# Staged norm and rotary chains for queries and keys, and Q/K projections scattered through the block of an eight-core hybrid layer

## The chip, the cores and the metric

The kernel runs on all 8 cores of one Trainium2 chip, each core on one of 8 batch entries, without traffic between cores. The metric is the time on the device of the slowest core. The profile lists the cores as two dies of four. In some executions, of nine of the fourteen kernels here, cores of one die (of both in the last run of the changed kernel) ran at a lower granted TensorE clock and the time was longer: in one run of the changed kernel four cores had 0.853 to 0.859 and took 2738.1 to 2774.8 us, the other four 0.972 to 0.976 and 2513.1 to 2524.3 us. Such runs are called slow, and only fast runs are compared. Names below: PE is TensorE, ACT is ScalarE, DVE is VectorE, POOL is GpSimd.

## The reference, cut to what matters

```python
h = _rmsnorm(x, g_mix)                                   # x: (8, 4096, 1024) float32
z = einsum(h, w_in)                                      # B_c | C_c | V_c | Q | K | V_a | gate_c | gate_a
y_c = (B_c * causal_dwconv3(C_c * V_c)) @ w_conv_out
q = _apply_rope(_rmsnorm(q, q_norm), cos, sin)           # per sub-head of 64; the same for k
o = (softmax(q1 k1) - lam * softmax(q2 k2)) @ v          # 4 heads, chunk-causal
y_a = (_rmsnorm(o, sub_norm) * (1 - lam_init)) @ w_attn_out
x = x + (sigmoid(gate_c) * y_c + sigmoid(gate_a) * y_a) @ w_o
x = x + SwiGLU(_rmsnorm(x, g_ffn))                       # 1024 -> 2816 -> 1024
```

## The kernel before

A core walks through 8 tiles of 512 tokens. For tile j it does conv and gates, w_o, the Q/K/V projection of tile j+2, FFN up and FFN down. The attention of tile j+1 is woven in as steps: two score matmuls, one exponential on ACT, eight P·V matmuls, spread evenly over the other matmuls. "Unit" means one PSUM bank's worth of projection (8 matmuls); there are 3 such banks (`psD`), used in rotation. Work that must wait for another engine is put off by `defer(n, f)`: f is put into the engines' instruction streams at the end of the n-th unit, counting the present one. In the trace what stands behind a wait in an engine's stream waits too: near 1402 us of the kernel before, ACT stands 2.81 us for a result of VectorE, and a ready activation and exponential behind it start only at 1404.3 and 1404.7 us. So the place in the stream is what this change is about.

The chain of one Q or K unit, and the order of the block:

```python
    act(lambda: A.activation(out=scr[:, s1, 0:512], in_=psD[bk][:], func=AF.Square), [("ps", bk)], [("scr", s1)])
    dve(lambda: V.tensor_tensor(
        out=s23, in0=ps3, in1=tabs[:, 2 * qk, t, :].unsqueeze(1).to_broadcast([128, 8, 64]), op=ALU.mult),
        [("ps", bk), ("tab", qk)], [("scr", s2)])
    dve(lambda: V.tensor_reduce(out=ss8, in_=s13, axis=AX.X, op=ALU.add), [("scr", s1)], [("ss8", pb)])
    dve(lambda: V.tensor_scalar(out=ss8, in0=ss8, scalar1=1.0 / 64, scalar2=EPS, op0=ALU.mult, op1=ALU.add),
        [("ss8", pb)], [("ss8", pb)])
    pool(lambda: G.tensor_tensor(out=rs8, in0=ss8, in1=mhalf[:], op=ALU.pow), [("ss8", pb), "mhalf"], [("rs8", pb)])
    sw = psD[bk][:].rearrange("p (g two d) -> p g two d", g=8, two=2)[:, :, ::-1, :]
    tb = tabs[:, 2 * qk + 1, t, :].rearrange("p (two d) -> p two d", two=2)
    dve(lambda: V.tensor_tensor(
        out=scr[:, s1, 0:512].rearrange("p (g two d) -> p g two d", g=8, two=2), in0=sw,
        in1=tb.unsqueeze(1).to_broadcast([128, 8, 2, 32]), op=ALU.mult),
        [("ps", bk), ("tab", qk)], [("scr", s1)])
    pool(lambda: G.tensor_tensor(out=scr[:, s2, 0:512], in0=scr[:, s2, 0:512], in1=scr[:, s1, 0:512], op=ALU.add),
         [("scr", s1), ("scr", s2)], [("scr", s2)])
# [cut: fin = final product yq = s2 * rs8 on VectorE; tr = 4 transposes of yq into a bank, copied to qT or kT]
    defer(1, fin)
    defer(3, tr)

def proj_qkv(j, free):
# [cut: rotary tables, ones column of V]
    for hbs, kind in ((HB_Q, 0), (HB_K, 1), (HB_V, 2)):
        for t in range(4):
            bk = tm_unit(hbs, t, j)
            if kind < 2:
                qk_chain(j, kind, t, bk)
# [cut: V copied out by ScalarE]
            unit_end()
```

The end of a head of attention (its epilogue), after the products with PSUM on VectorE:

```python
for q in range(4):
    act(lambda q=q: A.activation(out=yq[:, yi, q * 128:(q + 1) * 128], in_=wv[:, q, :], func=AF.Square,
                                 accum_out=ss[:, q:q + 1]), [("scr", w)], [("yq", yi), ("ess", e)])
dve(...)    # [cut] ss / 128 + eps
pool(...)   # [cut] rs = ss ** -0.5
# [cut: fin = wv * rs on VectorE, tr = 4 transposes and a copy]
defer(1, fin)
defer(3, tr)
```

Of the kernel before, what the change touches and what calls it, by code (L numbers as in the profile page):

```python
# [154 lines left out]
def build_program():  # L155
# [8 lines left out]
    with contextlib.ExitStack() as es:  # L164
# [6 lines left out]
        NDB = 3  # L171
        psD = [es.enter_context(nc.psum_tensor("psD%d" % i, [128, 512], F32)) for i in range(NDB)]
# [30 lines left out]
        st8 = sb("st8", [128, 2, 24], F32)  # L203
# [12 lines left out]
        def program(S_):  # L216
# [6 lines left out]

            def new_scr():
                return rot("scr", NSCR)

            def new_bank():
                return rot("bank", NDB)

# [42 lines left out]
            def defer(n, fn):  # L272
                later.append([n, fn])
# [8 lines left out]

            def flush_later():
                while later:
                    later.pop(0)[1]()
# [6 lines left out]
            SEQ_A = list(range(0, 6))  # L292
            SEQ_C1 = list(range(6, 28))
            SEQ_C2 = list(range(28, NHB))
            wseq = [(0, b) for b in SEQ_A]
            for j in range(NST):
                wseq += [(j, b) for b in SEQ_C1]
                if j + 2 < NST:
                    wseq += [(j + 1, b) for b in SEQ_A]
                wseq += [(j, b) for b in SEQ_C2]  # L300
            NW = len(wseq)
            ring = {"issued": 0, "cast": 0, "used": 0, "rel": [False] * NW, "cur": {}, "wb": []}
# [18 lines left out]
            def pump():  # L321
                while ring["issued"] < NW:
                    k = ring["issued"]
                    p, b = wseq[k]
                    if is_f32(k):
                        if k - NSTG >= ring["cast"]:
                            break
                        i = k % NSTG
                        S_.dma("sp", [lambda: nc.sync.dma_start(
                            out=stg_view(i), in_=wblk_d[b].rearrange("p (h c) -> p h c", h=4))],  # L330
                            [], stg_keys(i), ("stg", i))
                    else:
                        if k >= NSLOT and not ring["rel"][k - NSLOT]:
                            break
                        sl = k % NSLOT
                        n = hbw(b)
                        S_.dma("sp", [lambda: nc.sync.dma_start(out=wring[:, sl, 0:n], in_=wsc_d[b][:, 0:n])],
                               [("wsc", b)], [("w", sl)], ("wr", sl))
# [8 lines left out]
            def cast(k):  # L347
                assert k == ring["cast"] and (k < NSLOT or ring["rel"][k - NSLOT]), k
                p, b = wseq[k]
                i, sl = k % NSTG, k % NSLOT  # L350
                sv = stg_view(i)
                dst = wring[:, sl, :].rearrange("p (h c) -> p h c", h=4)
                if k % 2 == 0:
# [3 lines left out]
                ring["cast"] += 1  # L357
                ring["wb"].append((b, sl))

            def ready(k):  # L360

                while ring["cast"] <= k and ring["cast"] < NW and is_f32(ring["cast"]):
                    cast(ring["cast"])
                    pump()
                    do_wb(1)

            def ahead(k):
                if k < NW and is_f32(k) and (k < NSLOT or ring["rel"][k - NSLOT]):
                    ready(k)

            def wuse(b):

                if b in ring["cur"]:
                    return ring["cur"][b] % NSLOT
                k = ring["used"]
                assert wseq[k][1] == b, (wseq[k], b)
                if is_f32(k):
                    ready(k)
                    ahead(k + 1)
                else:  # L380
                    do_wb(0)
                    while ring["cast"] < NW and ring["cast"] <= k:
                        ring["cast"] += 1
                pump()
                assert ring["issued"] > k
                ring["used"] += 1
                ring["cur"][b] = k
                return k % NSLOT

            def wfree(b):  # L390
                k = ring["cur"].pop(b)
                if any(w[0] == b for w in ring["wb"]):
                    do_wb(0)
                ring["rel"][k] = True
# [12 lines left out]
            def norm_pre(t):  # L407
# [5 lines left out]
                dve(lambda: V.tensor_scalar(out=ss, in0=ss, scalar1=1.0 / D, scalar2=EPS, op0=ALU.mult, op1=ALU.add),  # L413
                    [("ss", t)], [("ss", t)])
                pool(lambda: G.tensor_tensor(out=rs, in0=ss, in1=mhalf[:, 0:1], op=ALU.pow),  # L415
                     [("ss", t), "mhalf"], [("rs", t)])
                dve(lambda: V.tensor_scalar(out=xn[:, t, :], in0=src, scalar1=rs, scalar2=None, op0=ALU.mult),
                    [("xt", t), ("rs", t)], [("xn", t)])

            def norm_T(t, gcol0, dst, dkey):  # L420
                bk = new_bank()
                bv = bankbf(bk).rearrange("p (c k) -> p c k", c=8)
                for kc in range(8):
# [5 lines left out]
                    [("ps", bk), "cst"], [(dkey, t)])  # L429

# [89 lines left out]
            def qk_chain(j, qk, t, bk):  # L520
                s1, s2 = new_scr(), new_scr()
                pb = rot("st8", 2)
                yi = rot("yq", NYQ)
                ps3 = psD[bk][:].rearrange("p (g d) -> p g d", g=8)
                s13 = scr[:, s1, 0:512].rearrange("p (g d) -> p g d", g=8)
                s23 = scr[:, s2, 0:512].rearrange("p (g d) -> p g d", g=8)
                ss8, rs8 = st8[:, pb, 0:8], st8[:, pb, 8:16]
                act(lambda: A.activation(out=scr[:, s1, 0:512], in_=psD[bk][:], func=AF.Square), [("ps", bk)], [("scr", s1)])
# [3 lines left out]
                dve(lambda: V.tensor_reduce(out=ss8, in_=s13, axis=AX.X, op=ALU.add), [("scr", s1)], [("ss8", pb)])  # L532
                dve(lambda: V.tensor_scalar(out=ss8, in0=ss8, scalar1=1.0 / 64, scalar2=EPS, op0=ALU.mult, op1=ALU.add),  # L533
                    [("ss8", pb)], [("ss8", pb)])
                pool(lambda: G.tensor_tensor(out=rs8, in0=ss8, in1=mhalf[:], op=ALU.pow), [("ss8", pb), "mhalf"], [("rs8", pb)])  # L535
                sw = psD[bk][:].rearrange("p (g two d) -> p g two d", g=8, two=2)[:, :, ::-1, :]
                tb = tabs[:, 2 * qk + 1, t, :].rearrange("p (two d) -> p two d", two=2)
# [6 lines left out]

                def fin():
                    dve(lambda: V.tensor_tensor(
                        out=yq[:, yi, :].rearrange("p (g d) -> p g d", g=8), in0=s23,
                        in1=rs8.unsqueeze(2).to_broadcast([128, 8, 64]), op=ALU.mult),
                        [("scr", s2), ("rs8", pb)], [("yq", yi)])

                def tr():
                    b2 = new_bank()
# [6 lines left out]
                    else:  # L559
                        c0 = j * T + t * 128  # L560
                        act(lambda: A.copy(out=kT[:, :, c0:c0 + 128], in_=bv), [("ps", b2)], [("kT", j * 4 + t)])

                defer(1, fin)
                defer(3, tr)

            def proj_qkv(j, free):
                make_tabs(j)
                pool(lambda: G.memset(Vs[:, j * 4:j * 4 + 4, :].rearrange("p k (h d) -> p k h d", d=VW)[:, :, :, 128:129], 1.0),
                     [], [("V", j * 4 + t) for t in range(4)])
                for hbs, kind in ((HB_Q, 0), (HB_K, 1), (HB_V, 2)):  # L570
                    for t in range(4):
                        bk = tm_unit(hbs, t, j)
                        if kind < 2:
                            qk_chain(j, kind, t, bk)
                        else:
                            act(lambda t=t, bk=bk: A.copy(
                                out=Vs[:, j * 4 + t, :].rearrange("p (h d) -> p h d", d=VW)[:, :, 0:128],
                                in_=psD[bk][:].rearrange("p (h d) -> p h d", h=NH)), [("ps", bk)], [("V", j * 4 + t)])
                        unit_end()
                    if free:  # L580
                        wfree(hbs[0])
                        wfree(hbs[1])
# [7 lines left out]
            def attention_steps(j):  # L590
# [31 lines left out]
                def epilogue(h):  # L622
# [25 lines left out]
                    yi = rot("yq", NYQ)  # L648
                    for q in range(4):
                        act(lambda q=q: A.activation(out=yq[:, yi, q * 128:(q + 1) * 128], in_=wv[:, q, :], func=AF.Square,  # L650
                                                     accum_out=ss[:, q:q + 1]), [("scr", w)], [("yq", yi), ("ess", e)])
                    dve(lambda: V.tensor_scalar(out=ss, in0=ss, scalar1=1.0 / 128, scalar2=EPS, op0=ALU.mult, op1=ALU.add),  # L652
                        [("ess", e)], [("ess", e)])
                    pool(lambda: G.tensor_tensor(out=rs, in0=ss, in1=mhalf[:, 0:4], op=ALU.pow), [("ess", e), "mhalf"], [("ers", e)])  # L654

                    def fin():
# [3 lines left out]
                            [("scr", w), ("ers", e)], [("yq", yi)])  # L660

                    def tr():
                        b2 = new_bank()
                        bv = bankbf(b2)[:, 0:512]
                        for q in range(4):
# [4 lines left out]
                            [("ps", b2), "sn08"], [("onT", h)])  # L670

                    defer(1, fin)
                    defer(3, tr)
# [29 lines left out]
            def conv(j):  # L703
                jb = j % 2
                for half in range(2):
                    for i in range(3):
                        b = HB_CONV + half * 3 + i
                        sl = wuse(b)
                        for col in range(2):
# [5 lines left out]
                            elif i == 1:  # L715
                                act(lambda bk=bk, c4=c4: A.copy(out=cT[:, c4, :], in_=psD[bk][:]), [("ps", bk)], [("big", 16 + c4)])
                            else:
# [4 lines left out]
            def conv_taps(c4, bk):  # L722
# [5 lines left out]
                    [("ps", bk), ("big", 16 + c4)], [("scr", u)])  # L728
                dve(lambda: V.tensor_copy(halo[:, c4, :], scr[:, u, T:T + 2]), [("scr", u)], [("halo", c4)])
# [9 lines left out]
                    [("scr", y), ("big", 12 + c4)], [("big", 8 + c4)])  # L739

            def gated(j, hg, ho, br, dc):
# [9 lines left out]
                    [("ps", bk), "bgh"], [("scr", th)])  # L751
# [234 lines left out]
```

## Time and profile before

| | before |
|---|---|
| time, median of the first 3 runs | 2868.5 us (2850.1 to 2902.2; the last counts as slow) |
| profiled run, span of the slowest core | 2843.8 us |
| PE busy, idle | 2393.0, 450.8 us |
| mean granted PE clock | 0.930 |
| Q/K/V stages of tiles 1 to 5, time and PE idle | 311.1, 97 us |

A page's first section gives each engine's busy time and share; its second cuts the span into 40 slices, and a digit is the busy share in tenths. A line of waits reads: who waited, for whom, us in total, times, longest. A stretch line gives the stretch, its length, then per engine the busy time and the number of instructions, then granted clock, DMA share and GB/s. A timeline line gives start, duration, engine, source line and what it wrote and read; the bracket tells how long the engine had been idle and who ended it. The lines themselves stand in the prediction.

### The profile page before, as it was taken

Reading aid. Unit: us, or ns where it says so; the run is one execution under the profiler, and the core shown is the slowest. Engines: PE = TensorE matmul, PEld = TensorE weight load, DVE = VectorE, ACT = ScalarE, POOL = GpSimd, SP = SyncE. Lnnn points to the kernel's source line nnn. Section 1 sums busy time; section 2 is a strip of 40 time slices with the busy share of each in tenths; the row PEclk is TensorE's granted clock in tenths of the full one; section 3 lists DMA queues with packets and bytes.
Section 4 is the critical chain, followed back from the end, with each engine's and each line's share of the span. In section 5 each row is a group of like instructions: output and inputs, shape, how many; then the busy total and the mean of one; then the engine's idle time right before and its main releaser. Section 6 shows DMA issues by size and latency. Waiting matters only on the chain.

```text
span 2843.8 us, 41548 instructions; the slowest of 8 cores (2839.7 to 2843.8 us)
## 1 busy us (share of the span) xinstructions
PE 2393.0 (84%) x14080; PEld 1110.5 (39%) x14080; DVE 1159.1 (41%) x2138; ACT 1058.7 (37%) x1556; POOL 243.5 (9%) x239
## 2 busy tenths in 40 slices
PE   2566779886997879987899879998799988999989
PEld 1222334333443334433344334443344444444434
DVE  4445544445344443345333453334533333223444
ACT  2134244223323233332443334443355444555310
POOL 1310110003000020001100021000210000000000
PEclk9788799988999889998999999999999999999999
DMA  6336659851335222352234422244122332223333
GB/s 197 106 126 216 222 164 330 297 174 60 113 118 187 97 82 97 121 174 86 82 104 135 156 68 91 99 143 152 60 90 97 118 127 91 82 78 123 134 120 139
DMA packets 107245, 373.61 MB, mean 131 GB/s; under 512 B 10528, under 2 KB 11680, under 8 KB 103072
## 3 DMA queue, kind: packets, MB, share of 16 engines
q1 hardware_dynamic: 106320, 367.81, 38.6%
q10 hardware_dynamic: 720, 3.15, 0.4%
q8 instruction: 119, 1.95, 0.3%
q14 instruction: 86, 0.70, 0.1%
HBM read 320.58 MB, written 50.33 MB: 130 GB/s over the span
## 4 chain that ended last, share of the span: by engine, by line
PE 67%; DVE 13%; issue 8%; ACT 4%; POOL 4%; DMA 3%; DVEq 1%; ACTq 0%; POOLq 0%; SPq 0%
PE psD L817 20%; PE psD L698 12%; PE psO L617 10%; PE psD L844 9%; PE psS L600 6%; PE psD L515 4%; PE psD L764 4%; PE psD L791 3%; DMA kT<-wblk 2%; ACT yq L650 2%; POOL scr L542 2%; DVE scr L645 2%; DVE scr L529 2%; DVE st L532 1%; POOL small L415 1%
## 5 line engine op out<-in xcount | busy, mean ns | idle before, releaser
L606 ACT ACTIVATE Pb<-psS 128x1024 bf16<-128x1024 f32 (+1 forms) x576 | 548.1, 952 | 795.5 <-PE psS L600 774.8
L817 PE MATMUL psD<-hF,wring 128*128 128x512 bf16 x2816 | 666.3, 385 | 10.5 <-DVE hF L426 5.0
L698 PE MATMUL psD<-hT,wring 128*128 128x512 bf16 x1792 | 448.0, 395 | 15.9 <-DVE Pb L609 6.9
L817 PEld LDWEIGHTS psD<-hF,wring 128*128 128x128 bf16 x2816 | 267.0, 99 | 294.0 <-issue 30.1
L617 PE MATMUL psO<-Vs,Pb 128*128 128x129 bf16 x4224 | 351.7, 229 | 3.1 <-DVE Pb L609 3.1
L844 PE MATMUL psD<-wring,big 128*128 128x512 bf16 x1408 | 333.3, 383 | 8.3 <-DVE wring L356 7.7
L515 PE MATMUL psD<-wring,hT 128*128 128x512 bf16 x768 | 245.5, 468 | 76.2 <-DVE scr L538 46.2
L617 PEld LDWEIGHTS psO<-Vs,Pb 128*128 128x128 bf16 x4224 | 256.1, 101 | 123.6 <-issue 114.7
L803 DVE SCALAR_TENSOR_TENSOR xt<-psD,xt 128x512 f32<-128x512 f32 x256 | 176.2, 691 | 272.3 <-PE psD L844 214.7
L825 DVE SCALAR_TENSOR_TENSOR scr<-scr,psD 128x512 f32<-128x512 f32 x176 | 121.1, 688 | 371.9 <-ACT scr L823 345.0
L600 PE MATMUL psS<-qT,kT 64*128 64x512 bf16 (+3 forms) x1152 | 222.1, 382 | 59.0 <-ACT Pb L606 58.9
L698 PEld LDWEIGHTS psD<-hT,wring 128*128 128x128 bf16 x1792 | 176.0, 101 | 217.4 <-issue 47.3
L844 PEld LDWEIGHTS psD<-wring,big 128*128 128x128 bf16 x1408 | 132.7, 99 | 150.7 <-issue 19.5
L600 PEld LDWEIGHTS psS<-qT,kT 64*128 64x128 bf16 x1152 | 56.3, 93 | 315.5 <-issue 315.5
L829 DVE TENSOR_TENSOR big<-scr,psD 128x512 bf16<-128x512 f32 x176 | 121.0, 688 | 126.8 <-PE psD L817 123.0
L823 ACT ACTIVATE scr<-psD 128x512 f32<-128x512 f32 x176 | 104.7, 596 | 174.1 <-PE psD L817 171.8
L750 ACT ACTIVATE scr<-psD,bgh 128x512 f32<-128x512 f32 x128 | 87.5, 686 | 219.3 <-PE psD L698 216.8
L654 POOL TENSOR_TENSOR ep<-ep,mhalf 128x4 f32<-128x4 f32 x32 | 32.3, 1010 | 1453.5 <-DVE ep L652 1420.9
L515 PEld LDWEIGHTS psD<-wring,hT 128*128 128x128 bf16 x768 | 81.4, 114 | 175.1 <-issue 135.2
L791 PE MATMUL psD<-wring,big 128*128 128x512 bf16 x512 | 124.7, 392 | 7.5 <-DVE wring L356 3.6
L535 POOL TENSOR_TENSOR st<-st,mhalf 128x8 f32<-128x8 f32 x64 | 105.1, 1643 | 260.6 <-DVE st L533 260.6
L424 PE MATMUL psD<-ident,xn 128*128 128x128 bf16 x512 | 45.7, 245 | 91.4 <-DVE hT L426 29.3
(88 smaller groups left out, 1600.3 us busy)
## 6 DMA issues: line engine op xcount, KB each, us to landing
wring<-wsc SPq DMA_DIRECT2D x414, 512.0 KB, 3.3
kT<-wblk SPq DMA_DIRECT2D x32, 1024.0 KB, 10.9
wsc<-wring SPq DMA_DIRECT2D x62, 512.0 KB, 10.9
Vs<-wblk SPq DMA_DIRECT2D x30, 1024.0 KB, 11.0
xt<-x SPq DMA_DIRECT2D x60, 512.0 KB, 8.0
out<-xt SPq DMA_DIRECT2D x32, 512.0 KB, 3.6
wring<-wsc SPq DMA_DIRECT2D x14, 256.0 KB, 2.8
xt<-x ACTq DMA_DIRECT2D x4, 512.0 KB, 13.6
```

The lines of the kernel that those rows point to most:

```text
L515: mm(lambda kc=kc, k4=k4, wv=wv: nc.tensor.matmul(psD[bk][:], lhsT=hT[:, jb, kc, t * 128:(t + 1) * 128], rhs=wv[:, k4, :], start=(kc == 0) ...
L600: S_.op("pe", lambda n=n: nc.tensor.matmul(psS[:, n, 0:N], lhsT=kT[n * 64:(n + 1) * 64, h, kt * 128:(kt + 1) * 128], rhs=qT[n * 64:(n + 1) ...
L606: act(lambda: A.activation(out=Pb[:, pi, :, 0:N], in_=psS[:, :, 0:N], func=AF.Exp, scale=0.125), [("ps", "S")], [("P", pi)])
L617: S_.op("pe", lambda q=q, n=n, b=b, s=s: nc.tensor.matmul(psO[:, b, s * VW:(s + 1) * VW], lhsT=Pb[:, pi, n, (q - r) * 128:(q - r + 1) * 12 ...
L698: mm(lambda kc=kc: nc.tensor.matmul(psD[bk][:], lhsT=wv[:, kc, col * 128:(col + 1) * 128], rhs=hT[:, jb, kc, :], start=(kc == 0), stop=(kc ...
L764: mm(lambda kc=kc, rhs=rhs: nc.tensor.matmul(psD[b2][:], lhsT=wv[:, kc, (dc % 4) * 128:(dc % 4 + 1) * 128], rhs=rhs, start=(kc == 0), stop ...
L791: mm(lambda kc=kc, k4=k4, wv=wv, t=t, bk=bk: nc.tensor.matmul(psD[bk][:], lhsT=mixT[:, kc, t * 128:(t + 1) * 128], rhs=wv[:, k4, :], start ...
L803: dve(lambda: V.scalar_tensor_tensor(out=xt[:, t, c * 512:(c + 1) * 512], in0=psD[bk][:], scalar=0.5, in1=xt[:, t, c * 512:(c + 1) * 512], ...
L817: mm(lambda kc=kc, gu=gu, bk=bk, wv=wv: nc.tensor.matmul(psD[bk][:], lhsT=wv[:, kc, gu * 128:(gu + 1) * 128], rhs=hF[:, kc, :], start=(kc ...
L825: dve(lambda th=th, bk=bk: V.scalar_tensor_tensor(out=scr[:, th, 0:T], in0=scr[:, th, 0:T], scalar=1.0, in1=psD[bk][:], op0=ALU.add, op1=A ...
L829: dve(lambda th=th, bk=bk, fi=fi: V.tensor_tensor(out=big[:, fi, :], in0=scr[:, th, 0:T], in1=psD[bk][:], op=ALU.mult), [("scr", th), ("ps ...
L844: mm(lambda kc=kc, wv=wv, t=t, bk=bk: nc.tensor.matmul(psD[bk][:], lhsT=big[:, kc, t * 128:(t + 1) * 128], rhs=wv[:, (kc - k0) % 4, :], st ...
```

## The change

Its intent: no engine should reach an instruction in its stream before the instruction's input is ready. The Q/K chain, the head epilogue and the row norms are cut into stages that are put off by more units; Q and K units are scattered so that the banks are less pressed; the transposes of the next tile's rows go between w_o units. Banks and scratch are handed out from free lists. The core of the diff:

```diff
 def qk_chain(...):
-    act(square of the bank into s1)
     dve(s2 = bank * cos table)
-    dve(reduce s1);  dve(scale, eps);  pool(rs8 = pow)
     dve(s1 = swapped bank * sin table)
     pool(s2 = s2 + s1)
-    defer(1, fin)
-    defer(3, tr)
+    defer(ds[0], square)      # ACT, bank into s1, then the bank is free
+    defer(ds[1], stats)       # DVE reduce and scale, POOL pow
+    defer(ds[2], fin)
+    defer(ds[3], tr)          # ds = (1, 2, 4, 6); for tiles 0 and 1 (1, 2, 3, 4)
 # head epilogue
-    squares; stats; defer(1, fin); defer(3, tr)
+    defer(2, square); defer(3, stats); defer(5, fin); defer(6, tr)
 # row norms: norm_pre(t) -> norm_pre(t, 1, 2) in the gates, norm_pre(t, 2, 3) in w_o
+    if d2 == 0: mid(); fin()
+    else: defer(d1, mid); defer(d2, fin)
 # per tile
-    for t in range(4): norm_T(t, ...)                  # 32 transposes in a row
-    out_proj(j)
-    proj_qkv(j + 2, True); flush_later()
-    ffn(j)
+    out_proj(j, lambda t: norm_T(t, ...))              # 8 after each of the first 4 units
+    V units 0..3, Q units 0, 1 of tile j + 2
+    ffn(j, qk_more)       # Q units 2, 3 after chunks 2, 4; K units after chunks 7, 10, 13, 16
```

(Rewritten for reading; the free lists and the order of the weight loads that goes with the new places are cut.)

## The prediction

> **What bounds the kernel now.** I read the page first (busy shares, slices), then the waits view for who made TensorE (PE) wait, then the stretches view cut by stage, then the timeline inside the two worst places. The page:
>
> ```profile
> PE 2393.0 (84%) x14080; PEld 1110.5 (39%) x14080; DVE 1159.1 (41%) x2138; ACT 1058.7 (37%) x1556; POOL 243.5 (9%) x239
> ...
> PE   2566779886997879987899879998799988999989
> ...
> PEclk9788799988999889998999999999999999999999
> DMA  6336659851335222352234422244122332223333
> ```
>
> PE is the fullest engine by far; VectorE (DVE) and ScalarE (ACT) are at 41% and 37%, so neither has to be made faster, only out of PE's way. PE is idle 2843.8 - 2393.0 = 451 us, and the PEclk row shows that its clock is also cut in many slices. Who PE waits for, from the waits view:
>
> ```profile
> PE psD L666 <- DVE yq L657: 76.0, 19, 5.6
> PE psS L600 <- ACT Pb L606: 58.9, 25, 7.6
> PE psD L555 <- DVE scr L538: 54.2, 29, 3.4
> PE psD L515 <- DVE scr L538: 46.2, 16, 5.1
> PE psD L424 <- DVE hT L426: 29.3, 7, 21.4
> PE psD L424 <- DVE scr L538: 28.3, 8, 6.5
> ```
>
> L515 is the Q/K/V projection, L555 the transposes of finished Q/K, L538 the last read of the projection's PSUM bank by the norm/rotary chain: 54.2 + 46.2 + 28.3 = 129 us wait for that chain. L666 transposes an attention head's normed output: 76 us for the head's epilogue. L600 are the scores, which wait for the exponentials (58.9). The five stages of tile 3 (conv with gates, w_o, Q/K/V of tile 5, FFN up, FFN down), from the stretches view; columns are time, busy time with instruction count of PE, weight load, DVE, ACT, POOL, then granted clock and DMA:
>
> ```profile
> 1206.20:1297.50 91.30, 78.20 (x429) 36.22 (x427) 41.34 (x79) 30.45 (x51) 3.23 (x5) 0.94 0.51 175
> 1297.50:1317.70 20.20, 19.92 (x108) 8.60 (x109) 8.52 (x13) 7.19 (x9) 1.09 (x2) 0.92 0.21 63
> 1317.70:1379.60 61.90, 42.26 (x251) 19.92 (x250) 30.57 (x57) 22.79 (x33) 23.16 (x19) 0.83 0.14 48
> 1379.60:1493.80 114.20, 107.30 (x687) 50.52 (x686) 37.70 (x73) 50.56 (x76) 2.02 (x2) 0.99 0.32 107
> 1493.80:1551.50 57.70, 53.92 (x339) 25.33 (x338) 20.63 (x39) 18.32 (x26) 1.01 (x1) 0.97 0.33 110
> ```
>
> The Q/K/V stage is the sick one: 19.6 us idle of 61.9 and a clock of 0.83. The FFN beside it is 94% busy, with DVE at 33% and ACT at 44%: it has room to hide chains in. Inside the FFN the loss looks like this (PE's timeline):
>
> ```profile
> 1401.16 1.47 PE L817 MATMUL psD<-hF,wring 128*128 128x512 bf16 x6
> 1406.79 0.38 PE L666 MATMUL psD<-ident,yq 128*128 128x128 bf16 x4 [4.16 <-DVE yq L657]
> 1407.49 1.86 PE L817 MATMUL psD<-hF,wring 128*128 128x512 bf16 x4 [0.32 <-DVE scr L825]
> ```
>
> The transposes stand in PE's order three units after the epilogue, the epilogue takes longer, PE stands still 4.16 us, and then 4 matmuls take 1.86 us (0.47 each) where the steady pitch is 0.216 us (tile 7's chain of waits has 176 down-projection matmuls in 38.00 us).
>
> [...] granted shares are 0.5 and 1.0 only, and the first 8 projection matmuls after such a stop take 3.2 to 3.6 us (0.40 to 0.45 each). [...] at 1402 ACT waits 2.81 us for the epilogue's DVE result, and a ready gate activation and exponential stand behind it until 1404.3 and 1404.7. [...]
>
> **The change, part by part.** Arithmetic, matmul count and bytes stay; order and waits change.
>
> (a) *The Q/K chain* becomes stages. Before, per unit: ACT square 0.60, DVE cos product 0.69, reduce 0.68, scale 0.17, sin product 0.68 (may not start before the reduce has read the square), POOL power 1.64 and add 1.1, and DVE's final product waits for POOL in order (L546 lost 114 us of DVE so). The bank is held for square and four DVE steps; beside PE this loop turns in about 5 us a unit. Now the two DVE products come first, POOL adds, the square runs last and frees the bank, and reduce, final product and transpose come 1, 3 and 5 units later. From the durations the bank is held 0.69 + 0.68 + 1.1 + 0.6 plus hand-overs, about 3.5 us: not shorter. What helps is the other change:
>
> (b) *Placement.* The dense block of 4 Q and 4 K units is gone. V (one 0.59 us ACT copy each) and two Q units follow w_o, covering the FFN norm's latency; two Q and four K units go singly into the FFN, at least two chunks (four units) apart. Two units of 8 x 0.216 = 1.73 us plus an attention step cover the 3.5 us for which one of three banks is held. The 96 + 32 PE instructions of the stage still cost their warm time.
>
> (c) *Epilogue and row norms* staged (square 2, statistics 3, product 5, transposes 6 units later): ACT finds its input ready, PE finds yq ready. This aims at the 76 us, most of the 58.9 us, and the gaps after the row norm.
>
> (d) *Residual transposes* of tile j+2 go one by one between w_o units instead of 32 in a row behind 1.22 us evictions.
>
> (e) *Weight ring* slots and the float32 staging of tile 0 are handed out by free list. Before a bf16 reload amid tile 0 the staging must now run empty, twice.
>
> Sum. A floor for PE: 7808 matmuls of 512 columns x 0.216 = 1687; 576 attention steps, full ones 0.885 each (in the steady FFN 10 matmuls and a step take 3.045; 3.045 - 2.16), about 480 in all; 896 transposes x 0.056 = 50; 45 us before the first projection. Together 2262, so 582 us of the span is idle or half-clock. By part:
> - Tiles 1 to 5, Q/K/V stages: idle 21.7 + 19.7 + 19.6 + 18.2 + 17.8 = 97 (each stretch less PE's busy time in it, as 61.9 - 42.3 above); cold, (1 - granted clock) x time, with clocks of 0.78, 0.81, 0.83, 0.86 and 0.86: 53. I take 90% back, 135, less 0.5 us for each of 30 units for the new wait of rival 1: 120.
> - Tiles 1 to 5, the rest: the five tiles take 1719.8 with PE busy 1506.6 at 0.94, so 213 idle, less 97, is 116; cold 0.06 x 1719.8 = 103, less 53, is 50. Staging recovers, I choose, 60% and 75%: 107.
> - Tiles 6 and 7: 49 idle and 23 cold, no Q/K/V; 55%: 40.
> - Tile 0 with start (503.7 us, 147.5 idle): its Q/K/V of tiles 0 to 2 idles 85 us, but FFN and down move 314 and 304 GB/s at DMA shares of 0.98 and 0.91, so part of what PE gains there turns into waiting for weights. I take 80.
> Total 347, span 2843.8 - 347 = 2497. Unprofiled runs lie a little above the profiled one (2868.5 median against 2845.6), so I say **2520 us**, 12% less.
>
> **Rivals.** (1) *The square as a new wait*: it stands in ACT's order right behind its own unit and waits for POOL's add (0.69 + 0.68 + 1.1 = 2.5 us), with exponentials behind it; scores steps come every 3.0 us with 1.02 us of exponential, so a bad phase costs PE 1 to 2 us. For it: strict order; against: only 6 units a tile in the FFN, ACT at 44%. If it took 2 us at all 48 Q/K units of tiles 2 to 7 with half clock after it, some 100 to 150 us of the gain goes: 2640. (2) *Tile 0 is bound by transfers*, and the emptied staging adds 10 to 15 us at each reload: its gain shrinks to 20 or vanishes: 2580. [...] (4) *Gaps all close*: floor plus tile 0's transfers, about 2410.
>
> **Range and chances.** Rivals 1 and 2 together give about 2650; rival 4 gives 2410. Range 2420 to 2640. Same would need more than 80% of the gain to be lost: 0.05. Slower would need a new bound that no view shows: 0.02.
>
> **What would show it.** Right: PE's wait of L666 on the epilogue product under 15 us (was 76); waits on the Q/K chain's second product under 30 us (were 129); PE idle under 200 us and mean clock 0.97 or more (was 0.93); FFN stages of tiles 0 to 5 longer by about 15 us each, the stage between w_o and FFN down to about 20. Wrong: large waits of scores on exponentials or of exponentials behind the square in the FFN (rival 1); tile 0 still ending near 548 us with DMA shares of 0.9 (rival 2)[...].

## The result

The changed kernel is correct. Its four runs took 2526.5 and 2536.8 us (fast) and 2776.4 and 2825.3 us (slow: one die at a granted clock of 0.83 to 0.86, in the last run the other die too, at 0.90 to 0.91). The ratio of the fast runs is 0.885, interval 0.871 to 0.900. Ratios are the mean time of one kernel's fast runs over that of the other's in the same rounds, so they differ a little from the ratio of quoted medians. The predicted time was 2520.

The page of the changed kernel (core 0, of whose matmuls 264 have no record):

```profile
PE 2271.1 (90%) x13816; PEld 1076.3 (43%) x14080; DVE 1154.3 (46%) x2138; ACT 1047.5 (41%) x1556; POOL 257.8 (10%) x239
...
PE   2668778989999998989999999999999999999999
...
PEclk9789889999999999999999999999999999999999
```

The other engines' busy times have hardly moved; only PE's idle time and cut clock went. For all else I use core 1, whose records are complete: span 2521.4, PE busy 2287.6, idle 233.8, clock 0.974. Its waits, for those shown of before (there 76.0 for the head transposes, 58.9 for scores, 129 for the Q/K chain):

```profile
PE psS L652 <- ACT Pb L658: 24.0, 27, 3.8
PE psD L602 <- DVE yq L591: 14.4, 9, 3.0
PE psD L602 <- ACT scr L574: 10.9, 4, 4.1
PE psD L724 <- DVE yq L714: 8.9, 10, 3.3
```

L724 are now the head transposes, L652 the scores, L602 the Q/K transposes, L574 the chain's square, which frees the bank. Tile 3 in the same five stages:

```profile
1036.40:1112.70 76.30, 71.59 (x398) 33.25 (x397) 37.03 (x74) 30.46 (x51) 3.49 (x5) 1.00 0.56 196
1112.70:1134.30 21.60, 20.37 (x141) 9.85 (x140) 13.50 (x24) 8.69 (x13) 1.08 (x2) 1.00 0.33 105
1134.30:1150.90 16.60, 16.60 (x131) 8.82 (x130) 9.59 (x13) 8.10 (x11) 2.09 (x4) 1.00 0.34 118
1150.90:1282.90 132.00, 123.63 (x810) 59.14 (x808) 56.67 (x111) 62.16 (x96) 23.69 (x18) 0.99 0.30 100
1282.90:1335.20 52.30, 52.30 (x339) 24.67 (x338) 20.49 (x39) 18.32 (x26) 1.01 (x1) 1.00 0.36 122
```

The tile went from 345.3 to 298.8 us. The FFN grew by 17.8 us with the six units it took in, the Q/K/V stage shrank by 45.3, conv and gates by 15.0, FFN down by 5.4. (The 32 residual transposes, small PE instructions, moved from conv and gates into w_o, which grew by 1.4.) By part of the span (stretches of core 3 before, core 1 after):

| part | before | after | less | predicted less |
|---|---|---|---|---|
| until the first projection | 44.8 | 44.1 | 0.7 | 0 |
| tile 0 | 503.7 | 433.1 | 70.6 | 80 |
| tiles 1 to 5 | 1719.8 | 1503.0 | 216.8 | 227 |
| tiles 6 and 7 | 575.5 | 541.2 | 34.3 | 40 |
| span | 2843.8 | 2521.4 | 322.4 | 347 |

So the sizes by place were right. Whether the reasons were, this table cannot tell: chain order, placement, epilogue and row norms are mixed in each row.

### The profile page after: what moved, and what is told of

Same layout as the page of the kernel before. It is cut to its first block, busy times and chain, and to the rows that moved or that the text cites.

```text
span 2524.9 us, 41096 instructions; the slowest of 8 cores (2512.6 to 2524.9 us)
## 1 busy us (share of the span) xinstructions
PE 2271.1 (90%) x13816; PEld 1076.3 (43%) x14080; DVE 1154.3 (46%) x2138; ACT 1047.5 (41%) x1556; POOL 257.8 (10%) x239
## 4 chain that ended last, share of the span: by engine, by line
PE 76%; DVE 10%; issue 5%; ACT 3%; POOL 2%; DMA 2%; DVEq 0%; ACTq 0%; SPq 0%; POOLq 0%
PE psD L890 20%; PE psD L760 13%; PE psD L920 11%; PE psO L669 11%; PE psS L652 6%; PE psD L550 5%; PE psD L861 4%; PE psD L832 3%; POOL scr L570 2%; ACT Pb L658 1%; DVE scr L697 1%; PE psD L458 1%; DVE scr L563 1%; DVE scr L566 1%; DMA xt<-x 1%
## 5 line engine op out<-in xcount | busy, mean ns | idle before, releaser
L890 PE MATMUL psD<-hF,wring 128*128 128x512 bf16 x2712 | 662.4, 386 | 42.6 <-ACT wring L386 16.3
L760 PE MATMUL psD<-hT,wring 128*128 128x512 bf16 x1739 | 425.5, 385 | 13.6 <-DVE big L838 7.4
L669 PE MATMUL psO<-Vs,Pb 128*128 128x129 bf16 x4224 | 339.9, 223 | 6.6 <-DVE scr L697 5.4
L920 PE MATMUL psD<-wring,big 128*128 128x512 bf16 x1359 | 319.9, 379 | 9.4 <-DVE wring L388 6.6
L669 PEld LDWEIGHTS psO<-Vs,Pb 128*128 128x128 bf16 x4224 | 245.3, 99 | 122.2 <-issue 113.3
L652 PE MATMUL psS<-qT,kT 64*128 64x512 bf16 (+3 forms) x1152 | 215.5, 370 | 27.1 <-ACT Pb L658 24.2
L550 PE MATMUL psD<-wring,hT 128*128 128x512 bf16 x740 | 193.3, 397 | 21.2 <-DVE wring L388 11.9
L920 PEld LDWEIGHTS psD<-wring,big 128*128 128x128 bf16 x1408 | 131.6, 98 | 146.3 <-issue 12.7
L652 PEld LDWEIGHTS psS<-qT,kT 64*128 64x128 bf16 x1152 | 56.3, 93 | 271.2 <-issue 271.2
L896 ACT ACTIVATE scr<-psD 128x512 f32<-128x512 f32 x176 | 105.2, 598 | 145.4 <-PE psD L890 143.4
L861 PE MATMUL psD<-wring,big 128*128 128x512 bf16 x494 | 123.1, 387 | 12.4 <-DVE wring L388 7.3
L584 POOL TENSOR_TENSOR st<-st,mhalf 128x8 f32<-128x8 f32 x64 | 107.2, 1676 | 175.5 <-DVE st L582 157.3
L574 ACT ACTIVATE scr<-psD 128x512 f32<-128x512 f32 x64 | 38.2, 597 | 207.3 <-POOL scr L570 169.8
L570 POOL TENSOR_TENSOR scr<-scr 128x512 f32<-128x512 f32 x64 | 76.9, 1201 | 462.8 <-DVE scr L566 442.9
```

Source lines behind the costliest of these rows:

```text
L550: mm(lambda kc=kc, k4=k4, wv=wv: nc.tensor.matmul(psD[bk][:], lhsT=hT[:, jb, kc, t * 128:(t + 1) * 128], rhs=wv[:, k4, :], start=(kc == 0) ...
L652: S_.op("pe", lambda n=n: nc.tensor.matmul(psS[:, n, 0:N], lhsT=kT[n * 64:(n + 1) * 64, h, kt * 128:(kt + 1) * 128], rhs=qT[n * 64:(n + 1) ...
L669: S_.op("pe", lambda q=q, n=n, b=b, s=s: nc.tensor.matmul(psO[:, b, s * VW:(s + 1) * VW], lhsT=Pb[:, pi, n, (q - r) * 128:(q - r + 1) * 12 ...
L760: mm(lambda kc=kc: nc.tensor.matmul(psD[bk][:], lhsT=wv[:, kc, col * 128:(col + 1) * 128], rhs=hT[:, jb, kc, :], start=(kc == 0), stop=(kc ...
L861: mm(lambda kc=kc, k4=k4, wv=wv, t=t, bk=bk: nc.tensor.matmul(psD[bk][:], lhsT=mixT[:, kc, t * 128:(t + 1) * 128], rhs=wv[:, k4, :], start ...
L890: mm(lambda kc=kc, gu=gu, bk=bk, wv=wv: nc.tensor.matmul(psD[bk][:], lhsT=wv[:, kc, gu * 128:(gu + 1) * 128], rhs=hF[:, kc, :], start=(kc ...
```

## The experiments

All start from the changed kernel unless said otherwise, and all gave correct results. Twelve ran. Times are fast runs; chip 5 served eight of them, and had the kernel before at 2849.2 to 2852.4 us fast; chip 12 served the four of which the text says so. The changed kernel itself was not run again beside them. Differences are taken to its 2526.5 us or, on chip 12, to its profiled cores (2512.6 to 2524.9 us, middle 2522). That this carries over rests on the kernel before, whose cores in fast runs took 2833 to 2851 us on chip 5 and 2840 to 2844 us when it was first profiled; a difference of 10 us between runs of different days is therefore not read.

### Placement and order of the Q/K chain: three runs

The first takes the scattering back and keeps the staged chain.

```diff
-    V 0..3, Q 0, 1; then Q 2, 3 and K 0..3 inside ffn
+    for kind in (0, 1, 2):            # Q, K, V
+        for t in range(4): qkv_unit(j + 2, kind, t, DS1)
```

> The changed kernel, but the Q, K and V units of tile j+2 stand again in one block (4 Q, 4 K, 4 V) between w_o and the FFN; the staged Q/K chain and all other stagings stay. Theory A (placement opens the Q/K/V stage, staging the chain alone does not, since a bank is held about 3.5 us either way): the block has 45 to 55 us with 8 to 15 us of PE idle per tile and a cut clock, and the span is 2580 to 2620. Rival B (the order of the chain is what counts, the place is not): PE idle in the block under 3 us, span within 15 us of the changed kernel's 2522.

Measured: 2521.9 to 2523.9 us, ratio 0.885 (0.883 to 0.887): the same as the changed kernel. Tile 3's Q/K/V block and FFN, from the stretches view of this run:

```profile
1137.40:1176.20 38.80, 34.68 (x248) 17.48 (x247) 29.95 (x50) 19.55 (x29) 23.81 (x19) 0.96 0.24 82
1176.20:1284.20 108.00, 106.00 (x694) 50.13 (x692) 37.41 (x73) 51.21 (x78) 2.01 (x2) 1.00 0.34 113
```

The dense block idles 4.1 us, the FFN 2.0; scattered, the two idle 0 and 8.4. My theory A fell: the scattering moved a few us of waiting from the block into the FFN and gained nothing. Rival B put the idle at under 3 us, which also is not quite what came, but its span is met.

The second keeps the scattered places and puts the old chain there.

```diff
+    act(square); dve(cos product); dve(reduce); dve(scale); pool(pow); dve(sin product); pool(add)
-    defer(ds[0], square) ... defer(ds[3], tr)
+    defer(1, fin)
+    defer(3, tr)
```

> The changed kernel with the Q/K chain of before (square first on ScalarE, VectorE reduce and scale between the two products, final product at the unit's end, transposes two units later), at the new scattered places. Theory A (placement): little is lost, span 2525 to 2560, because the next units come from other work. Rival B (order of the chain): each of 48 scattered Q/K units stalls PE by 1.5 to 3 us through VectorE's wait for GpSimd, span 2600 to 2660.

Measured: 2636.1 to 2642.8 us, 113 more than the changed kernel. Its waits:

```profile
DVE yq L586 <- POOL scr L577: 150.4, 62, 2.7
PE psD L597 <- DVE yq L586: 81.6, 43, 4.9
```

That is in rival B's span. VectorE stands at the final product, which waits for GpSimd's power and add, and PE stands at the transposes two units later. Scattering does not help, since the stream distance between producer and user is as short as before.

The third undoes both.

```diff
+    dense block and old chain, as in the two edits above
```

> Both parts of the Q/K change undone (dense block and old chain); epilogue, row norms, residual transposes and weight ring stay as changed. The prediction's term for the Q/K/V stages (120 us in tiles 1 to 5, some 15 to 40 in tile 0) makes this 2660 to 2690. If the two parts overlap fully, it is no slower than the worse of the two undone singly.

Measured: 2632.8 to 2634.8 us, 108 more than the changed kernel, no slower than the second, and below the expected 2660 to 2690. So the whole Q/K change is worth some 110 us, all of it by the staged chain. VectorE's timeline in the block of tile 3 shows what the old chain waits for (L584 is the final product, L563 and L570 the two products that read the bank):

```profile
1235.28 0.69 DVE L584 TENSOR_TENSOR yq<-scr,st 128x512 bf16<-128x512 f32 x1 [2.54 <-POOL scr L575]
1235.89 0.68 DVE L563 TENSOR_TENSOR scr<-psD,tabs 128x512 f32<-128x512 f32 x1
...
1237.35 0.68 DVE L570 TENSOR_TENSOR scr<-psD,tabs 128x512 f32<-128x512 f32 x1
1240.56 0.69 DVE L584 TENSOR_TENSOR yq<-scr,st 128x512 bf16<-128x512 f32 x1 [2.52 <-POOL scr L575]
1241.17 0.68 DVE L563 TENSOR_TENSOR scr<-psD,tabs 128x512 f32<-128x512 f32 x1
```

One turn takes 1240.56 - 1235.28 = 5.28 us, of which VectorE waits about 2.5 for GpSimd. The next unit's first read of its bank (L563) stands behind that wait, though its bank may be long full.

### Is it that one wait? One edit

Theory C came from these lines. The fourth run starts from the third and changes two numbers.

```diff
-    defer(1, fin)
-    defer(3, tr)
+    defer(2, fin)
+    defer(4, tr)
```

> The kernel with dense block and old chain (2634) with one edit: the chain's final product on VectorE and its transposes come one unit later (2 and 4 instead of 1 and 3); square first, reduce and scale between the products stay. Theory C (formed after the dense block with the staged chain ran as fast as the scattered one: the cost was VectorE's wait for GpSimd in its order, 12 us of a 58 us block, which stands in front of the next unit's first product): most of the 110 us comes back, span 2530 to 2570, and VectorE's wait for GpSimd in the block falls from 12 us to under 3. Rival D (square-first order and the statistics between the products are what holds the bank): span stays above 2600.

Measured: the two fast runs took 2541.7 and 2544.8 us (two more were slow; no interval could be formed), 91 less than without the edit. The waits of VectorE for GpSimd's sum in these two runs, first without, then with the edit:

```profile
DVE yq L584 <- POOL scr L575: 105.3, 56, 2.7
```

```profile
DVE yq L584 <- POOL scr L575: 11.2, 5, 2.6
```

The block of tile 3 went from 58.3 us to 44.6:

```profile
1199.30:1257.60 58.30, 41.30 (x251) 19.66 (x250) 28.80 (x50) 21.52 (x31) 24.25 (x19) 0.82 0.16 54
```

```profile
1144.60:1189.20 44.60, 35.73 (x251) 17.14 (x250) 29.33 (x50) 21.00 (x31) 25.11 (x19) 0.96 0.20 69
```

In this block VectorE's wait for GpSimd's sum fell from 12.1 us to none; a wait of the final product for a GpSimd memset of V's ones column stayed (1.8 us here; 19.7 us over the kernel before the edit, 14.6 after). Both the wait and the span are within the expectation. The edit moves the transposes too, so one may ask whether PE gained there. It did not gain much: its waits for the final product at the Q/K transposes went from 22.1 to 12.7 us, its waits for the last read of a bank (L570) from 102.1 to 49.0. Theory C is shown for most of the 108 us: about 91. The square-first order and the statistics between the products, rival D, account for at most the rest.

The traces also tell by which way the wait reached PE. For the 48 Q/K units of tiles 2 to 7, the medians of the time from the end of a unit's last matmul to the end of the last read of its bank, and of the part of it before the first product (core 0; core 1 of the changed kernel):

| place, chain | bank held, us | of it before the first product | VectorE's wait for the sum or power | time |
|---|---|---|---|---|
| dense, old | 5.7 | 3.5 | 105.3 | 2634.5 |
| scattered, old | 3.0 | 0.9 | 150.4 | 2639.5 |
| dense, old with the product one unit later | 3.8 | 1.4 | 11.2 | 2543.2 |
| dense, staged | 4.3 | 0.7 | 20.5 | 2523.8 |
| scattered, staged | 3.5 | 0.1 | 14.1 | 2526.5 |

Scattering alone did free the banks early, as the prediction wanted, but with the old chain PE then lost its time at the transposes (81.6 us against 22.1 in the dense block). The two slow rows are those in which VectorE waits over 100 us, and not those in which the bank is held longest; the 20 us between the other three are not told by either.

### The square that waits for GpSimd (rival 1 of the prediction)

In the changed kernel the square overwrites the scratch that GpSimd's add reads, so it waits for the add. Near 1258 us of core 1, first ACT's timeline, then PE's:

```profile
1257.08 0.60 ACT L574 ACTIVATE scr<-psD 128x512 f32<-128x512 f32 x1 [5.34 <-POOL scr L570]
1257.57 1.02 ACT L658 ACTIVATE Pb<-psS 128x1024 bf16<-128x1024 f32 x1
```

```profile
1253.19 2.33 PE L890 MATMUL psD<-hF,wring 128*128 128x512 bf16 x10
1258.73 0.39 PE L652 MATMUL psS<-qT,kT 64*128 64x512 bf16 x2 [3.21 <-ACT Pb L658]
```

ACT stands 5.34 us at the square (a head epilogue held VectorE, so the products came late), an exponential whose scores were done at about 1253.3 stands behind it, and PE waits 3.21 us for that. The edit squares at once, into the unit's `yq` buffer in bf16, which costs no memory:

```diff
+    yi = alloc("yq")
+    act(yq[yi] = square of the bank)          # before the two products
-    defer(ds[0], square)
     stats: reduce yq[yi] instead of s1; fin overwrites yq[yi]
```

> The changed kernel (scattered) with the Q/K square written in bf16 to the unit's yq buffer, at once, so that it no longer waits for GpSimd's add and ScalarE's order is not blocked; bank free after the second product. Theory (rival 1 of the prediction is real but small: some 8 us of PE idle per FFN of tiles 0 to 5 come from the square): FFN idle falls from 8 to under 3 us a tile, span 2480 to 2500. Rival: those gaps have another cause, span within 10 us of 2522.

Measured: 2486.1 to 2488.8 us, ratio 0.873 (0.871 to 0.874). The FFN of tile 3 takes 127.1 us and idles 4.0, from 132.0 and 8.4:

```profile
1129.70:1256.80 127.10, 123.13 (x809) 59.28 (x807) 57.69 (x111) 62.06 (x95) 24.15 (x18) 0.99 0.32 104
```

Rival 1 was real and worth some 35 us: that is within the expectation. The FFN's idle fell to 2.1 us in tile 4, but not below 3 in every tile. The edit does two things at once: ACT no longer stands at the square, and the bank is free after the second product (held a median of 2.1 us, from 3.5). PE's wait of the scores for exponentials went from 24.0 to 3.4 us and its wait for the square as last reader of a bank from 18.8 to none, while that for final products at the Q/K transposes rose from 14.4 to 27.7; no run separates the two. The FFN of tile 0 gained most (127.4 to 116.2 us), and PE's wait there for weight casts, which stand in ACT's order too, went from 16.3 to 5.6 us.

The same edit with the dense block:

> Dense block with the staged chain and the early bf16 square. The dense block's 4 to 7 us of idle per tile waited for the square, so they close: span 2475 to 2495, equal to the scattered one with the same square within 10 us. If the scattered placement has a value of its own once the square is out of the way, this is slower by over 15 us.

Measured: 2516.1 to 2523.4 us. It missed: the dense block did not gain, and so the scattered one is some 33 us faster with this edit. So the scattering has a value, but only once the square is out of the way. In tile 3 the block still idles 6.0 us; over the kernel PE waits 29.8 us for final products at its transposes, which is hardly more than the scattered version's 27.7, and 10.0 for V's copies, which the scattered version does not show. The traces place the difference: some 21 us lie in tiles 1 to 5 and 13 in tile 0; in each of tiles 1 to 5 PE idles 4.8 to 8.4 us from w_o to the FFN, against 1.0 to 1.7, and the first product starts 2.0 us after its unit's end, against 0.8. So the units follow each other faster than VectorE takes up their chains; no run tests that.

### The head epilogue

```diff
-    defer(2, square); defer(3, stats); defer(5, fin); defer(6, tr)
+    square(); stats(); defer(1, fin); defer(3, tr)
```

> The changed kernel with the head epilogue of attention as before: squares and statistics at once, final product at the unit's end, transposes two units later. Theory (epilogue staging removed the 76 us wait of the transposes and most of the 58.9 us of scores on exponentials): span 2600 to 2630, the transposes wait 60 to 80 us again. Rival: with PE's other waits gone the units between are shorter in time, so the wait is even longer, over 90 us; or the placement of the rest hides it and it is under 20.

Measured: 2674.1 to 2676.5 us, 150 more than the changed kernel, and more than expected. Then only half of it was undone, the squares and statistics:

```diff
-    defer(2, square); defer(3, stats); defer(5, fin); defer(6, tr)
+    square(); stats(); defer(5, fin); defer(6, tr)
```

> The changed kernel with one half of the epilogue staging undone: the four squares and the statistics at once, the final product and the transposes still 5 and 6 units later. With the whole staging undone the kernel took about 2672; there PE waited 66 us for the product and 70 us in the scores for exponentials. If these are two separate costs (ScalarE blocked by the squares that wait for VectorE; PE blocked by the early transposes), this one keeps the exponential part: scores wait 50 to 75 us, transposes under 15, span 2570 to 2620. If all of it came from the early transposes, span within 15 us of 2522.

This ran on chip 12; in the profiled run the cores of one die had a mean granted clock of 0.945 to 0.948, those of the other 0.955 to 0.957. The four cores of the latter, undisturbed die took 2630.5 to 2637.0 us, some 113 more than the changed kernel's cores (the full undoing: 147 more by cores). Waits of the full undoing, then of the half:

```profile
PE psS L652 <- ACT Pb L658: 70.3, 33, 7.5
PE psD L724 <- DVE yq L714: 65.9, 15, 6.2
```

```profile
PE psS L652 <- ACT Pb L658: 58.8, 30, 7.5
PE psD L724 <- DVE yq L714: 8.4, 6, 5.6
```

Waits and time do not tell the same story. By PE's waits the two causes look equal; by time the squares and statistics at once carry about 113 us, and the early product and transposes, which in the kernel before showed the larger number, the other 35. Which engine carries the 113 is not separated: in the half undoing ACT stands 110.6 us at the squares (33.6 in the changed kernel), and VectorE 67.1 us at the statistics behind them (9.1). The two halves can overlap, since PE standing at one gives ACT time to catch up; only this one order of undoing was run. The expectation's span (2570 to 2620) was too low.

### Row norms and residual transposes

```diff
-    norm_pre(t, 1, 2); norm_pre(t, 2, 3); 8 transposes after each of the first 4 w_o units
+    norm_pre(t) at once; 32 transposes in a row before w_o; row loads at once too
```

> The changed kernel with the row norms unstaged (square, statistics and product at once, four rows in a row) and the 32 residual transposes of tile j+2 again in one run before w_o. Expected from the kernel before, where gates waited 12 us for the row-norm statistics, and transposes 29 us for hT evictions and 19 for the product: 25 to 60 us slower than the changed kernel, span 2547 to 2582. Rival: below 10 us, other work hides it.

Measured: 2608.9 to 2614.4 us, 84 more, against an expected 25 to 60. Waits of this run:

```profile
DVE xn L444 <- POOL small L440: 48.5, 55, 1.7
PE psD L458 <- DVE hT L460: 46.6, 7, 21.9
```

Again VectorE stands for GpSimd's power (5.3 us in the changed kernel). With the transposes alone put back:

> The changed kernel with only the 32 residual transposes of tile j+2 back in one run before w_o (row norms stay staged). Undoing both together cost 86 us. From that trace one run of transposes has 4.1 us of idle in tile 3 where the changed kernel has about 1, and the cut clock after it: if the transposes carry half or more, this is 2560 to 2575 in span; if the row norms carry nearly all (ScalarE's four squares in a row and VectorE's waits behind them), it is under 2535.

On chip 12, the undisturbed die (mean clock 0.965 to 0.968; two cores of the other had 0.955 and 0.956) took 2544.5 to 2555.5 us, some 31 more than the changed kernel's cores: a little over a third of the 84, between the two expectations. By subtraction the row norms, with the place of the row loads, carry about 53; they were not undone alone.

### Two misses in tile 0

The condition that a bf16 reload waits until the float32 staging is empty was loosened:

```diff
-    if not ring["slots"] or ring["fcast"] < ring["fissued"]: break
+    if len(ring["slots"]) <= ring["fissued"] - ring["fcast"]: break
```

> The changed kernel, with one condition of the weight ring loosened: a bf16 reload amid the float32 stream of tile 0 may be issued as soon as more slots are free than staged blocks wait for their cast, instead of when the staging is empty. Rival 2 of the prediction (the emptied staging costs 10 to 15 us at each of two reloads): the stages of tile 0 from w_o to the FFN's end (174 us in the changed kernel) get 10 to 25 us shorter, span about 2500 to 2512. If tile 0's FFN is held by the float32 stream itself (transfers or casts), nothing changes: within 5 us of 2522.

On chip 12 every run had a pair of cores or more with a lower mean clock (in the fast runs, of 2548.8 to 2555.4 us, 0.961 to 0.963, the other cores 0.971 to 0.974). The cores with undisturbed clock took 2527.3 to 2533.2 us in the profiled run, no less than the changed kernel's 2512.6 to 2524.9, and tile 0 from w_o to the FFN's end was 177 us (174 in the changed kernel). The emptied staging is not what holds tile 0.

Last, a version meant to beat both: the early square, this loosened condition, the four row-norm squares spread over four gates, and no flush after the first two tiles' K units.

> A version meant to beat both: the changed kernel with the early bf16 square (2488 by itself), the loosened reload condition, the four row-norm squares spread over the first four gates instead of in a row (3 us of PE idle at the start of the gates in each of 6 tiles), and no flush of the deferred work after the K units of tiles 0 and 1 (two runs of three transposes that wait 3 us each, some 18 us). If these add, 2488 less 10, 15 and 15: 2440 to 2465.

On chip 12: 2482.3 to 2506.6 us, ratio 0.870 (0.859 to 0.880); cores 2469.9 to 2480.8, where the early square alone had 2470.9 to 2487.2 on chip 5. So of the hoped 40 us some 5 came. The first stage did get shorter by 15 us (106.0 to 90.6), but conv and w_o after it took 7 more and FFN down of tile 0 7 more; spreading the squares changed little (conv and gates of all tiles: 661.0 against 659.9 us). Both versions beat the kernel before and the changed one; which of the two is faster stays open.

### What no run undid

Some parts of the change were never undone by themselves: the other order of Q, K and V units in tiles 0 and 1, the free lists, the attention steps left over being flushed one gate earlier, and the earlier place of the rotary tables. One number can be split: the first projections, up to the first conv unit, went from 128.8 to 106.8 us, 22 of the 70.6 us that tile 0 gained. In the two runs with the old chain they take 119.9 and 121.9 us, so 13 to 15 of the 22 are the staged chain's; the rest stays open.

## Why the prediction was right or wrong

**Time.** Right: 2520 predicted, 2526.5 and 2536.8 measured in fast runs. That it came so close is in part luck. The sum gave a span of 2497, and the profiled span is 2521.4 to 2524.9: the gain was 25 us too large. Against this stood 23 us for runs that lie above the profiled one, and the profiled run took only 1.6 us more than its slowest core's span (2526.5 against 2524.9). The two errors cancel. Also, the shares of idle and cold time to be won back (90, 60, 75 and 55%) were chosen, not derived. And rivals 1 and 2 together, as the prediction sizes them (120 and 60 us), give 2700 and not 2650.

**The bound.** Right: PE's idle time and cut clock went from 451 us and 0.930 to 234 us and 0.974, and no other engine's busy time changed by much.

**Part (a) and (b), the Q/K term of 120 us plus a share of tile 0.** The size was near (108 to 113 measured for all tiles, by undoing), the reason was wrong. The step that failed: "the bank is held 0.69 + 0.68 + 1.1 + 0.6 plus hand-overs, about 3.5 us: not shorter. What helps is the other change", meaning placement. I had summed the durations of the chain's instructions. From the timelines of PE, DVE and ACT, matching each Q/K unit of tiles 2 to 7 with its chain, the bank was held a median of 6.2 us before, of which 4.0 passed before the first product began; in the changed kernel it is 3.5, as estimated, with 0.1 before the first product. And the hold was the wrong quantity: scattered with the old chain it is 3.0 us, and the kernel is 113 us slower. What made the difference stood in my own sentence, "DVE's final product waits for POOL in order (L546 lost 114 us of DVE so)", and I did not carry it into the sum. Moving that product, with its transposes, one unit later regained 91 us; placement by itself regained nothing.

**Part (c), epilogue and row norms.** Right in kind, undersized, and split wrongly. Undoing the epilogue costs 150 us, where the prediction put all its other terms for tiles 1 to 7 at 107 + 40. I took PE's wait for the early transposes (76 us) as the main item; the half undoing shows the larger share, 113 us, in squares and statistics that come too early in the orders of ACT and VectorE; ACT's wait I had listed second. Row norms cost about 53 more, by subtraction, which no term had by itself. What kept the total right is that the singly undone parts, 108 + 150 + 84 = 342, are close to the 322 gained, and that the prediction was built from idle time by place, not by cause.

**Part (d).** About 31 us, not sized separately.

**Part (e) and rival 2.** The staging that must run empty did not show: loosening it gained nothing. Tile 0 gained 70.6 of the 80.

**Rival 1.** Right: it cost some 35 us. For tiles 1 to 5, where the text took "0.5 us for each of 30 units" (15 us), the early square gained some 28 us (1503.0 to 1474.6), so the term was about half of it.

**The clock.** In the traces of the kernel before and of the changed one, both of fast runs, all cores have granted shares of 0.5 and 1.0 only. The slow runs of the changed kernel, at mean clocks down to 0.83, were not traced. In the kernel before (core 3, from the first projection on) the stretches of one share last multiples of 3.41 us, and the clock falls 78 times. In 61 of them PE had been busy for 11 to 46% of the 3.41 us before, in the other 17 for 6% or less. It came back after 3.41 us in which PE was busy for 79% or more. 52 of the 78 half-clock stretches last 3.41 us, each an estimated 1.7 us of lost clock (half of 3.41); the other 26 last 6.8 to 17.1 us.

**The signs.** Head transposes under 15 us: 8.9. Q/K chain under 30: no wait on the second product among the large ones, 18.8 on the square that took its place as the bank's last reader (10.9 + 4.1 + 3.8) and 14.4 on the final product. FFN longer by about 15: 17.8 in tile 3. Stage after w_o down to 20: 16.6. Idle under 200: missed at 234, of which about 40 lies before the first projection and 100 in tile 0, where I had expected less to remain.

## What to carry to other kernels

When a busy-enough engine is idle in short pieces, look for the instruction at which an engine waits for a third one with work standing behind it (here VectorE for GpSimd, about 2.5 us a turn), and put that instruction one unit later in the stream before moving whole blocks of work: two changed numbers gave 91 us here and a new placement none, until the square too was out of the way (then 33). Count a buffer's hold from the producer's end to the last reader's end in the timeline, not as the sum of its readers' durations, and look whether the consumer waits for the buffer at all or for the chain's result. And when a chain is reordered, ask of its new last step which engine's stream it now blocks: the square behind the add cost 35 us until it was given its own buffer.
